# An even layer's pooling as products with band matrices, wider value chunks, work moved to ScalarE, parameters begun later

## The chip, the cores and the metric

The kernel runs on one core of a Trainium2 chip. Its time is the device time of one execution in microseconds (us), and the figure for a kernel is the median over runs. The core has a matrix engine (TensorE, PE in the rows; PEld is its loading of stationary matrices), VectorE (DVE), ScalarE (ACT), GpSimd (POOL) and SyncE (SP), which issues most transfers. Each engine works through its own list of instructions in order and waits on semaphores for the others. On-chip data lies in SBUF; matmuls write to PSUM.

## The reference, cut to what matters

The program is an even layer, an odd layer, a mixing layer (a Fourier part and a state space model, the ssm) and a mixture of experts. The change lies in the even layer, and in the preparation of the ssm's parameters, which runs in the background of the even layer.

```python
def even_layer(...):          # z = rmsnorm(h) @ ev_w_in, split in columns
    pooled = pool_mixer(za, ev_pool_w, scale)     # za: 768 columns
    ret = retention(rq, rk, rv)                   # 4 heads, keys of 128, values of 192
    mem = mem_attention(xq, mem_n, w_mem_kv)
    h + (concat(pooled, ret, mem) * silu(gate)) @ ev_w_out

def pool_mixer(u, w_grp, scale):                  # groups of 192 channels
    for gi, w in enumerate((2, 4, 8, 16)):        # mean over the last w tokens, minus the token
        lo = max(t + 1 - w, 0)
        outs.append((cs[:, 1:, sl] - cs[:, lo, sl]) / (t + 1 - lo) - uf[..., sl])
    y = einsum('bsgc,gcd->bsgd', stack(outs), w_grp) * scale

def retention(q, k, v):                           # q, k rotated by position
    att = (q @ k.T) * decay                       # causal, per head
    o = att @ v                                   # in the reference: in chunks with a carried state
    o = (o - mean(o)) * rsqrt(var(o) + EPS)       # over the 192 columns of a head
```

## The kernel before

The 512 tokens are four blocks of 128 (`NB`). Every fp32 operand is held as a pair, a rounded high part and the remainder: `split` (L300 and L301) takes the high part by a copy on ACT and the remainder by a subtraction on DVE, and `scaled_split` (L310 and L311) does so with a factor for each partition. A product of two pairs is three matmuls (`mm3`, L315 to L317). Weights stream in by `weight_piece`: SP fetches up to 1024 columns' worth (`wraw`), ACT makes the high part (L344), and DVE the low part (L346); while `share` is 2, in the retention, POOL makes the low part of every second piece.

`proj_t` makes 128 output channels for all 512 tokens (24 matmuls of 512 columns, stationary operand: weights). `proj_n` makes token-major results, block after block, each with one PSUM tile of the four named "mm"; two more are "acc" and two "tr".

The retention (`even_ret`) goes through four heads: rotary query, the products of the head before, rotary key, values, one step of an earlier output projection (`self.wait()`), scores. The values of a head are 192 columns, so `values(h)` runs four times. `products` collects two PSUM "acc" tiles, takes mean and variance on DVE, and normalises four parts from PSUM, each by L768 on DVE.

The pooling (`even_pool`) makes six tiles of 128 channels by `proj_t`, and for each one DVE adds shifted copies (L826: 2, 4, 8, 16 tokens), scales and subtracts (L831), mends the first 16 tokens (L834 and L835) and splits the result; then come gate tiles and the group products.

`ssm_params` is a generator. Each `tick()`, at the start of every projection, takes one of its steps: exponentials and angles on DVE (L1097 to L1142), and for eight groups of parameters products on POOL (L1292 to L1297) with DVE subtractions between them, right-hand sides `crhs` (L1281 to L1285 on POOL) and small matmuls (L1259). It is assigned to `self.bg` before the memory branch. What a step issues stands in each engine's list between the layer's own instructions: a scheduler places it by the order in which the program issues it and by the buffers that come free.

Of the kernel before, what the change touches and what calls it, by code (L numbers as in the profile page):

```python
# [12 lines left out]
ALU = mybir.AluOpType  # L13
# [11 lines left out]
GROUPS = 1 + BLOCKS // 2  # L25
SH_RET = 2
# [6 lines left out]
def chunk_list(spans, width=128):  # L33
# [10 lines left out]
    "za": chunk_list([(0, 768)]),  # L44
    "rq": chunk_list([(768, 1280)]),
    "rk": chunk_list([(1280, 1792)]),
    "rv": chunk_list([(1792, 2560)], 192),
# [60 lines left out]
POOL_WIN = (2, 4, 8, 16)  # L108
POOL_BLOCKS = []
# [15 lines left out]
def const_arrays():  # L125
# [13 lines left out]
    pc = np.zeros((P, 6, 16), np.float32)  # L139
    t = np.arange(16)  # L140
    for tl in range(6):
        for q in range(P):
            w = POOL_WIN[(tl * 128 + q) // 192]
            pc[q, tl] = np.float32(1.0) / np.minimum(t + 1, w).astype(np.float32)
    c["pcnt"] = pc
# [96 lines left out]
class K:  # L242
# [126 lines left out]
    def proj_n(self, w, name, i, u, evac, nblk=NB):  # L369
# [4 lines left out]
        for b in range(nblk):  # L374
            out = self.ps()
            s = slice(b * P, (b + 1) * P)
            for k in range(w.kt):
                self.mm3(out[:, :n], tuple(x[:, s] for x in u[k]), wt[k], k == 0, k == w.kt - 1)
            evac(b, out[:, :n], n)

# [271 lines left out]
    def even(self, before_end=None, aside=None):  # L652
# [53 lines left out]
    def even_ret(self, w, u, wo):  # L706
# [40 lines left out]
        def products(h):  # L747
# [32 lines left out]
        for h in range(4):  # L780
# [6 lines left out]
            values(h)  # L787
            self.wait()
            scores(h)
        self.wait(2)  # L790
# [4 lines left out]
    def even_pool(self, w, u):  # L795
        nc, a = self.nc, self.a
        v = nc.vector
        npb = len(POOL_BLOCKS)
        pw = []
        for b0 in range(0, npb, 4):  # L800
            n = min(4, npb - b0)
            hi, lo = self.split_new(self.load(a["ev_pw"][:, b0:b0 + n], [P, n, P]), [P, n, P])
            pw += [(hi[:, z], lo[:, z]) for z in range(n)]
        pcnt = self.load(a["pcnt"], [P, 6, 16])
        pooled, ys = {}, []
        done = 0

        def window(tl):
            o = self.proj_t(w, "za", tl, u)
            x = self.s([P, 16 + T])  # L810
            v.memset(x[:, :16], 0.0)
            v.tensor_tensor(x[:, 16:], o, self.rfull, ALU.mult)
            pend = []
            for q0 in (0, 64):
                win = POOL_WIN[(tl * 128 + q0) // 192]
                if pend and pend[0][2] == win:
                    pend[0] = (0, 128, win)
                else:
                    pend.append((q0, q0 + 64, win))
            res = self.s()  # L820
            cur, lvl, q0 = x, 1, 0
            maxw = max(p[2] for p in pend)
            while lvl < maxw:
                nxt = self.s([P, 16 + T])
                s0 = 2 * lvl - 1
                v.tensor_tensor(nxt[q0:, s0:], cur[q0:, s0:], cur[q0:, s0 - lvl:16 + T - lvl], ALU.add)  # L826
                lvl *= 2
                cur = nxt
                for (p0, p1, win) in list(pend):
                    if win == lvl:  # L830
# [1346 lines left out]
```

## Time and profile before

| | us |
|---|---|
| median of 3 runs | 2358.47 |
| lowest and highest | 2357.61, 2365.06 |
| profiled execution, its own time | 2362.91 |
| span of its trace | 2361.1 |
| PE busy in the span | 2131.4 |
| DVE, ACT, POOL busy | 1109.2, 661.2, 422.7 |

The span runs from the first to the last instruction. PE is busy for 90% of it. The even layer takes about the first 500 us; the rest is the other layers, which the change leaves as they are. The mean granted clock of PE in the profiled execution is 0.964 of full speed. The granted clock of a stretch (PEclk) is a mean of times at 1.2 and at 2.4 GHz; at the lower level a matmul takes about twice as long. A matmul's own duration overlaps with the next one's, so what a matmul costs in a stream is the distance from its start to the next one's start.

### The profile page before, as it was taken

How to read it: one execution, taken by the hardware profiler on the slowest of the kernel's cores; microseconds unless marked ns; L12 is line 12 of the kernel's file. 1: busy time of each engine (PE TensorE's matmuls, PEld its weight loads, DVE VectorE, ACT ScalarE, POOL GpSimd, SP SyncE). 2: the span in 40 equal slices, each digit the busy share in tenths (PEclk: the TensorE clock that was granted, in tenths of full speed). 3: DMA queues.
4: the chain of work that ended last, by engine and by line, in shares of the span. 5: the costliest groups of instructions: out<-in, count | busy, mean ns of one | idle time of the engine just before them, and what ended most of it. 6: DMA issues, size and time to landing. Idle time of an engine off the chain costs nothing. (4 is left out here: it accounts for less than half of the span.)

```text
span 2361.1 us, 30316 instructions
## 1 busy us (share of the span) xinstructions
PE 2131.4 (90%) x11350; PEld 1408.9 (60%) x11350; DVE 1109.2 (47%) x2229; ACT 661.2 (28%) x1289; POOL 422.7 (18%) x465
## 2 busy tenths in 40 slices
PE   7989998999999999999999988998787878887966
PEld 7878887787788888879777764433232323232311
DVE  7787869675446656666662634231111111111203
ACT  6623222344535645643224321000000000000001
POOL 1235755210014433421220210000000000000000
PEclk9989999899999999999999989999999999999988
DMA  5213334454232122114253489899999999999996
GB/s 183 94 59 108 116 100 138 141 167 152 72 102 64 38 73 72 43 59 137 90 163 108 152 333 381 339 392 426 427 427 426 427 426 427 427 427 427 427 426 252
DMA packets 110689, 545.85 MB, mean 231 GB/s; under 512 B 13664, under 2 KB 14605, under 8 KB 62410
## 3 DMA queue, kind: packets, MB, share of 16 engines
q1 hardware_dynamic: 105690, 529.14, 57.8%
q0 software_dynamic: 4528, 13.67, 1.7%
q8 instruction: 92, 1.51, 0.3%
q10 hardware_dynamic: 320, 1.05, 0.1%
q14 instruction: 59, 0.48, 0.1%
HBM read 530.70 MB, written 15.20 MB: 231 GB/s over the span
## 5 line engine op out<-in xcount | busy, mean ns | idle before, releaser
L2013 PE MATMUL mps<-ew,xt 128*32 128x512 f32 (+1 forms) x2048 | 383.4, 645 | 85.1 <-DMA ew<-in_w_up 47.9
L315 PE MATMUL ps<-uh,wh 128*128 128x512 f32 (+1 forms) x728 | 294.7, 405 | 7.8 <-ACT uh L310 7.0
L317 PE MATMUL ps<-uh,wl 128*128 128x512 f32 (+1 forms) x728 | 289.9, 398 | 5.1 <-DVE wl L346 5.1
L344 ACT ACTIVATE wh<-wraw 128x1024 fp32r<-128x1024 f32 (+5 forms) x187 | 186.8, 999 | 379.1 <-PE ps L316 267.5
L316 PE MATMUL ps<-ul,wh 128*128 128x512 f32 (+1 forms) x728 | 289.4, 398 | 0.5 <-DVE ul L311 0.5
L2013 PEld LDWEIGHTS mps<-ew,xt 128*32 128x32 f32 (+1 forms) x2048 | 86.5, 118 | 326.3 <-issue 170.7
L346 DVE TENSOR_TENSOR wl<-wraw,wh 128x1024 fp32r<-128x1024 f32 (+4 forms) x172 | 218.7, 1272 | 52.7 <-ACT wh L344 51.4
L2036 PE MATMUL mps<-ew,s 128*32 128x512 f32 (+1 forms) x960 | 173.9, 608 | 25.7 <-DMA ew<-in_w_down 13.9
L2099 POOL TENSOR_TENSOR ew<-x,ew 128x512 f32<-128x512 f32 x4 | 5.0, 1290 | 908.1 <-DMA ew<-in_w_down 908.1
L315 PEld LDWEIGHTS ps<-uh,wh 128*128 128x128 f32 (+1 forms) x728 | 137.2, 188 | 43.3 <-ACT uh L310 7.0
L317 PEld LDWEIGHTS ps<-uh,wl 128*128 128x128 f32 (+1 forms) x728 | 136.9, 188 | 40.0 <-DVE wl L346 6.0
L316 PEld LDWEIGHTS ps<-ul,wh 128*128 128x128 f32 (+1 forms) x728 | 137.2, 188 | 31.7 <-DVE ul L311 1.0
L1990 PE MATMUL mps<-s,hn 128*128 128x256 f32 (+1 forms) x576 | 135.0, 386 | 2.6 <-DVE s L1931 2.6
L1990 PEld LDWEIGHTS mps<-s,hn 128*128 128x128 f32 x576 | 104.4, 198 | 53.3 <-issue 33.5
L315 PE MATMUL ps<-yh,wh 128*128 128x512 f32 x320 | 130.8, 411 | 1.9 <-DVE s L311 1.9
L317 PE MATMUL ps<-yh,wl 128*128 128x512 f32 x320 | 128.4, 401 | 4.0 <-DVE wl L346 4.0
L2036 PEld LDWEIGHTS mps<-ew,s 128*32 128x32 f32 (+1 forms) x960 | 49.0, 113 | 137.6 <-issue 79.7
L2018 DVE SCALAR_TENSOR_TENSOR s<-mps,tab,s 128x512 f32<-128x512 f32 x17 | 12.8, 750 | 248.7 <-issue 153.3
L316 PE MATMUL ps<-yl,wh 128*128 128x512 f32 x320 | 129.0, 403 | 0.2
L1998 DVE TENSOR_SCALAR xt<-mps,gperm 128x256 f32<-128x256 f32 (+1 forms) x36 | 16.8, 468 | 237.2 <-PE mps L2013 198.3
L310 ACT ACTIVATE s<-mps,tab 128x512 fp32r<-128x512 f32 x34 | 23.4, 687 | 346.7 <-PE mps L2036 332.5
L311 DVE SCALAR_TENSOR_TENSOR s<-mps,tab,s 128x512 fp32r<-128x512 f32 x34 | 25.5, 751 | 188.4 <-ACT s L310 187.6
(517 smaller groups left out, 3962.7 us busy)
## 6 DMA issues: line engine op xcount, KB each, us to landing
ew<-in_w_gate SPq DMA_DIRECT2D x128, 1024.0 KB, 19.5
ew<-in_w_up SPq DMA_DIRECT2D x128, 1024.0 KB, 19.5
ew<-in_w_down SPq DMA_DIRECT2D x128, 1024.0 KB, 19.5
wraw<-in_od_w SPq DMA_DIRECT2D x44, 512.0 KB, 3.6
wraw<-in_ev_w SPq DMA_DIRECT2D x34, 512.0 KB, 3.5
wraw<-in_b_w SPq DMA_DIRECT2D x24, 512.0 KB, 3.5
b<-in_od_w SPq DMA_DIRECT2D x32, 256.0 KB, 4.3
wraw<-in_ev_wo SPq DMA_DIRECT2D x16, 384.0 KB, 3.3
```

The source lines that it names most:

```text
L310: self.nc.scalar.activation(hi, src, AF.Copy, scale=col)
L311: self.nc.vector.scalar_tensor_tensor(lo, src, col, hi, ALU.mult, ALU.subtract)
L315: mm(out, l[0], r[0], start=start, stop=False)
L316: mm(out, l[0], r[1], start=False, stop=False)
L317: mm(out, l[1], r[0], start=False, stop=stop)
L344: nc.scalar.activation(hi, raw, AF.Copy)
L346: (nc.gpsimd if on_pool else nc.vector).tensor_tensor(lo, raw, hi, ALU.subtract)
L1990: nc.tensor.matmul(tp[:, k * n:k * n + n], self.hn[:, b, k0 + k], one, start=i == 0, stop=i == len(sel) - 1)
L1998: nc.vector.tensor_scalar(t_[:, k], o, g, None, ALU.mult)
L2013: nc.tensor.matmul(o[rs], xt[k][:, c0 + z * m:c0 + z * m + m], self.expert_rhs(w[i][z], k, 512, 0, 512), start=k == 0, stop=k == KD - 1)
L2018: nc.vector.scalar_tensor_tensor(act, h[1], r, act, ALU.mult, ALU.mult)
L2036: self.nc.tensor.matmul(y[hf][rs], at[:, k, rs], self.expert_rhs(w[-1][r], k, D, hf * 512, 512), start=k == 0, stop=k == 3)
```

## The change

Values and pooling inputs come in chunks of 384 columns (two each, instead of four of 192 and six of 128). The new `proj_wide` keeps four PSUM tiles open, one for each token block, and takes each piece of weights through all of them; values are made at heads 0 and 2 alone, for two heads at a time. The pooling no longer adds shifted copies: a constant 128 by 144 matrix for each window holds the weights of the mean minus the token, and token-major inputs are multiplied by it (96 matmuls in all). The normalisation after the retention's products runs on ACT, as do the copies into `crhs` and the square in `sincos`. `ssm_params` is assigned to `self.bg` after the scores of head 0.

```diff
+BG_FROM = 0
...
-    "za": chunk_list([(0, 768)]),
+    "za": chunk_list([(0, 768)], 384),
     "rq": chunk_list([(768, 1280)]),
     "rk": chunk_list([(1280, 1792)]),
-    "rv": chunk_list([(1792, 2560)], 192),
+    "rv": chunk_list([(1792, 2560)], 384),
...
-    c["pcnt"] = pc
+    c["band"] = np.stack([np.stack([
+        np.where((j >= p) & (j < p + w), np.float32(1.0) / n.astype(np.float32), np.float32(0.0)) - (j == p)
+        for n in (np.full_like(j, w), np.minimum(j + 1, w))], 1) for w in POOL_WIN], 1).astype(np.float32)
...
+    def proj_wide(self, w, name, i, u, evac):
+
+        self.tick()
+        n = w.off[name, i][1]
+        step = 1024 // n
+        outs = [self.ps("acc"), self.ps("acc"), self.ps(), self.ps()]
+        for k0 in range(0, w.kt, step):
+            wt = self.weight_piece(w.src(name, i, k0, k0 + step)[0], step, n)
+            for k in range(k0, k0 + step):
+                for b in range(NB):
+                    self.mm3(outs[b][:, :n], tuple(x[:, b * P:b * P + P] for x in u[k]), wt[k - k0], k == 0,
+                             k == w.kt - 1)
+            self.tick()
+        for b in range(NB):
+            evac(b, outs[b][:, :n], n)
...
-        self.bg = aside and aside()
         self.fills.append(self.add_out(wo, 12, self.mem_branch(w, u, kv, 1, first)))
         self.share = SH_RET
-        self.even_ret(w, u, wo)
+        self.even_ret(w, u, wo, aside)
...
-            vp = [self.pair([P, 2, 192]) for _ in range(2)]
-            v[h] = [tuple(x[:, b % 2] for x in vp[b // 2]) for b in range(NB)]
+
+            vp = [self.pair([P, 2, 192]) for _ in range(NB)]
+            for j in range(2):
+                v[h + j] = [tuple(x[:, j] for x in vp[b]) for b in range(NB)]
 
             def evac(b, o, n):
-                self.scaled_split(*v[h][b], o, self.rcol[:, b:b + 1])
-            self.proj_n(w, "rv", h, u, evac)
+                self.scaled_split(*(x.rearrange("p j d -> p (j d)") for x in vp[b]), o, self.rcol[:, b:b + 1])
+            self.proj_wide(w, "rv", h // 2, u, evac)
...
             r = self.rsqrt(rr, [P, NB])
+            mr = self.small([P, NB], "ret_mr")
+            nc.vector.scalar_tensor_tensor(mr, mv[:, :, 0], -1.0, r, ALU.mult, ALU.mult)
             for b in range(NB):
-                nc.vector.tensor_scalar(rn[h // 2][b][:, h % 2 * 192:h % 2 * 192 + 192], outs[b], mv[:, b, 0:1],
-                                        r[:, b:b + 1], ALU.subtract, ALU.mult)
+                nc.scalar.activation(rn[h // 2][b][:, h % 2 * 192:h % 2 * 192 + 192], outs[b], AF.Identity,
+                                     bias=mr[:, b:b + 1], scale=r[:, b:b + 1])
...
                 gated(0)
-            values(h)
+            if h % 2 == 0:
+                values(h)
             self.wait()
             scores(h)
+            if h == BG_FROM:
+                self.bg = aside and aside()
         self.wait(2)
         products(3)
         self.wait(2)
...
-        pcnt = self.load(a["pcnt"], [P, 6, 16])
...
-        def window(tl):
-            o = self.proj_t(w, "za", tl, u)
-            x = self.s([P, 16 + T])
-            v.memset(x[:, :16], 0.0)
-            v.tensor_tensor(x[:, 16:], o, self.rfull, ALU.mult)
...
-            while lvl < maxw:
-                nxt = self.s([P, 16 + T])
-                s0 = 2 * lvl - 1
-                v.tensor_tensor(nxt[q0:, s0:], cur[q0:, s0:], cur[q0:, s0 - lvl:16 + T - lvl], ALU.add)
-                lvl *= 2
...
-                    if win == lvl:
-                        v.scalar_tensor_tensor(res[p0:p1], cur[p0:p1, 16:], 1.0 / win, x[p0:p1, 16:], ALU.mult,
-                                               ALU.subtract)
-                        hd = self.small([P, 16], "pool_h")
-                        v.tensor_tensor(hd[p0:p1], cur[p0:p1, 16:32], pcnt[p0:p1, tl], ALU.mult)
-                        v.tensor_tensor(res[p0:p1, :16], hd[p0:p1], x[p0:p1, 16:32], ALU.subtract)
...
-            pooled[tl] = self.split_new(res)
+        mm = nc.tensor.matmul
+        for c in range(2):
+            zp = [self.pair([P, 384]) for _ in range(NB)]
+
+            def evac(b, o, n):
+                self.scaled_split(*zp[b], o, self.rcol[:, b:b + 1])
+            self.proj_wide(w, "za", c, u, evac)
...
+            band = [self.split_new(self.load(a["band"][:, 2 * c + j], [P, 2, BAND]), [P, 2, BAND]) for j in range(2)]
             self.wait()
+            for t in range(3):
+                pooled.append(self.pair())
+                for q0, q1, j in ((0, P, t // 2),) if t != 1 else ((0, 64, 0), (64, P, 1)):
+                    o = self.ps()
+                    hi, lo = band[j]
+                    for b in range(NB):
+                        l, o_, n = tuple(x[:, t * P:t * P + P] for x in zp[b]), o[:, b * P:], min(BAND, T - b * P)
+                        if b == 0:
+                            self.mm3(o_[:, :n], l, (hi[:, 1], lo[:, 1]), True, False)
+                        else:
+                            mm(o_[:, 16:n], l[0], hi[:, 0, 16:n], start=False, stop=False)
+                            mm(o_[:, :16], l[0], hi[:, 0, :16], start=False, stop=False)
+                            mm(o_[:, :n], l[1], hi[:, 0, :n], start=False, stop=b == NB - 1)
+                    self.split(*(x[q0:q1] for x in pooled[t]), o[q0:q1])
+                self.tick()
+            for t in range(3 * c, 3 * c + 3):
+                g = self.gate_tile(w, t, u)
                 op = self.ps("acc")
...
+                need = [b for b in POOL_BLOCKS if b[1] == t]
+                for n, (i, _) in enumerate(need):
+                    self.mm3(op, pw[i, t], pooled[i - 3 * c], n == 0, n == len(need) - 1)
...
-        nc.vector.tensor_tensor(c, h, h, ALU.mult)
-        nc.vector.tensor_scalar(c, c, -2.0, 1.0, ALU.mult, ALU.add)
+        nc.scalar.activation(c, h, AF.Square)
+        nc.scalar.activation(c, c, AF.Copy, bias=1.0, scale=-2.0)
...
-                g_.tensor_copy(crhs[ds_, 0, :, d], cm[ds_, 0, gs])
-                g_.tensor_scalar(crhs[ds_, 1, :, d], cm[ds_, 1, gs], -1.0, None, ALU.mult)
+                nc.scalar.activation(crhs[ds_, 0, :, d], cm[ds_, 0, gs], AF.Copy)
+                nc.scalar.activation(crhs[ds_, 1, :, d], cm[ds_, 1, gs], AF.Copy, scale=-1.0)
```

The instruction lists move with it. In the first, on DVE, the stretch around the evacuation of the first values before (L311 with 128x192 out of PSUM; L1107, L1098, L1099, L1213, L1225 and L1142 belong to the parameters):

```order
L1141 TENSOR_TENSOR s_1333<-s_1332 128x256
L311 SCALAR_TENSOR_TENSOR s_1328<-ps_1352,rcol_338,s_1327 128x192
L1142 TENSOR_SCALAR s_1333<-s_1333 128x256
L1226 TENSOR_TENSOR pc_1077<-s_1333,s_1236 128x256
L311 SCALAR_TENSOR_TENSOR s_1328<-ps_1379,rcol_338,s_1327 128x192
L311 SCALAR_TENSOR_TENSOR s_1330<-ps_1406,rcol_338,s_1329 128x192
L1213 TENSOR_TENSOR s_1460<-x_702,idx_677 128x288
L1105 TENSOR_SCALAR s_1464<-s_1460 128x288
L1098 TENSOR_SCALAR s_1463<-s_1464 128x288
L1099 TENSOR_SCALAR s_1463<-s_1463 128x288
L1107 SCALAR_TENSOR_TENSOR s_1464<-s_1463,s_1464 128x288
```

and now (L310 is the same line of `scaled_split`, L528 the output projection's addition, L756 the scores' decay):

```order
L300 TENSOR_TENSOR s_1183<-s_1176,s_1182 128x512
L310 SCALAR_TENSOR_TENSOR s_1187<-ps_1194,rcol_338,s_1186 128x384
L310 SCALAR_TENSOR_TENSOR s_1189<-ps_1195,rcol_338,s_1188 128x384
L310 SCALAR_TENSOR_TENSOR s_1191<-ps_1196,rcol_338,s_1190 128x384
L345 TENSOR_TENSOR wl_1594<-wraw_1591,wh_1593 128x1024
L310 SCALAR_TENSOR_TENSOR s_1193<-ps_1197,rcol_338,s_1192 128x384
L528 TENSOR_TENSOR h_104<-ps_1332,h_104 128x512
L528 TENSOR_TENSOR h_106<-ps_1346,h_106 128x512
L756 TENSOR_TENSOR s_1366<-ps_1362,s_1360 128x512
L300 TENSOR_TENSOR s_1369<-s_1366,s_1368 128x512
L756 TENSOR_TENSOR s_1376<-ps_1372,s_1360 128x384
```

The parameters' instructions that stood between the evacuations are gone from this place; the four evacuations follow each other with one weight piece between them.

The second is POOL at one group of parameters, before (`crhs`, then the products; DMA rows are transfers that POOL issues):

```order
L1281 MEMSET crhs_2950 128x256
L1284 COPY crhs_2950<-bc_1854 64x4x16
L1285 TENSOR_SCALAR crhs_2950<-bc_1854 64x4x16
L1284 COPY crhs_2950<-bc_1854 64x4x16
L1285 TENSOR_SCALAR crhs_2950<-bc_1854 64x4x16
L1292 TENSOR_TENSOR mat_2956<-pc_1077,bb_934 128x8x4x16
L1295 TENSOR_TENSOR mat_2957<-ps_1078,bb_934 128x8x4x16
L1274 DMA ssm_win_665<-s_2865 128x512
L1274 DMA ssm_win_665<-s_2873 128x512
L346 TENSOR_TENSOR wl_3113<-wraw_3110,wh_3112 128x768
L1293 TENSOR_TENSOR s_2958<-ps_1078,bb_934 128x8x4x16
```

and now (line numbers are one lower):

```order
L1280 MEMSET crhs_3293 128x256
L1280 MEMSET crhs_3459 128x256
L1291 TENSOR_TENSOR mat_3465<-pc_1887,bb_1727 128x8x4x16
L1294 TENSOR_TENSOR mat_3466<-ps_1888,bb_1727 128x8x4x16
L1292 TENSOR_TENSOR s_3301<-ps_1888,bb_1727 128x8x4x16
L1295 TENSOR_TENSOR s_3302<-pc_1887,bb_1727 128x8x4x16
L1296 TENSOR_TENSOR mat_3300<-mat_3300,s_3302 128x512
L1291 TENSOR_TENSOR s_3354<-pc_1887,bc_2248 128x8x4x16
L1292 TENSOR_TENSOR s_3356<-ps_1888,bc_2248 128x8x4x16
L1294 TENSOR_TENSOR s_3355<-ps_1888,bc_2248 128x8x4x16
L1295 TENSOR_TENSOR s_3357<-pc_1887,bc_2248 128x8x4x16
```

The four copies into `crhs` and the transfers and the weight piece that stood between the products are not there; nine products of two groups follow each other.

## Rows read from the trace of the kernel before

**Rows 1.** Page, busy time of the engines, share of the span, instructions.

```profile
PE 2131.4 (90%) x11350; PEld 1408.9 (60%) x11350; DVE 1109.2 (47%) x2229; ACT 661.2 (28%) x1289; POOL 422.7 (18%) x465
```

**Rows 2.** Windows; from:to, length, busy us of each engine, PEclk, DMA.

```profile
110.00:160.00 50.00, 42.96 (x235) 36.63 (x234) 41.60 (x91) 12.35 (x21) 10.59 (x7) 0.90 0.24 75
160.00:210.00 50.00, 48.16 (x274) 42.15 (x273) 43.70 (x82) 12.85 (x21) 20.42 (x16) 0.97 0.24 75
260.00:310.00 50.00, 45.76 (x264) 39.36 (x263) 35.80 (x69) 14.05 (x23) 37.16 (x38) 0.90 0.35 116
340.00:380.00 40.00, 33.03 (x161) 26.57 (x160) 38.91 (x42) 8.71 (x13) 25.66 (x30) 0.96 0.32 106
420.00:460.00 40.00, 40.00 (x184) 32.86 (x183) 25.05 (x45) 11.77 (x18) 17.62 (x29) 0.87 0.57 154
```

**Rows 3.** Timeline of PE; start, us, instruction, [idle before it, releaser].

```profile
43.09 0.35 PE L315 MATMUL ps<-wh,s 128*128 128x256 f32 x1 [2.17 <-DVE th L1132]
...
141.63 0.69 PE L315 MATMUL ps<-s,s 128*128 128x384 f32 x1 [4.12 <-DVE s L311]
...
294.77 3.62 PE L1259 MATMUL ps<-crhs,mat 128*128 128x32 f32 x16 [4.02 <-DVE s L768]
...
374.77 0.50 PE L317 MATMUL ps<-yh,wl 128*128 128x512 f32 x1 [4.02 <-DVE wl L346]
...
416.52 1.58 PE L875 MATMUL ps<-s,rel 33*12 33x512 f32 x2 [2.26 <-issue]
```

**Rows 4.** Timeline of DVE around the first values' evacuation.

```profile
134.82 2.54 DVE L1107 SCALAR_TENSOR_TENSOR s<-s,s 128x288 f32<-128x288 f32 x1
...
138.33 2.92 DVE L1113 SCALAR_TENSOR_TENSOR s<-s,s 128x288 f32<-128x288 f32 x6
141.17 0.41 DVE L311 SCALAR_TENSOR_TENSOR s<-ps,rcol,s 128x192 fp32r<-128x192 f32 x1
```

**Rows 5.** Timeline of DVE and of POOL, 341 and 366 us.

```profile
341.23 7.95 DVE L831 SCALAR_TENSOR_TENSOR s<-s,s 128x512 f32<-128x512 f32 x1
...
366.38 8.34 DVE L346 TENSOR_TENSOR wl<-wraw,wh 128x768 fp32r<-128x768 f32 x1
...
366.51 1.07 POOL L1293 TENSOR_TENSOR s<-ps,bb 128x512 f32<-128x512 f32 x1
...
372.85 1.05 POOL L1296 TENSOR_TENSOR s<-pc,bc 128x512 f32<-128x512 f32 x1
```

**Rows 6.** Timeline of PE, matmuls following each other.

```profile
115.85 0.25 PE L315 MATMUL ps<-wh,uh 128*128 128x192 f32 x1
...
123.75 0.27 PE L317 MATMUL ps<-wh,ul 128*128 128x192 f32 x1
...
145.24 0.63 PE L316 MATMUL ps<-ul,wh 128*128 128x512 f32 x1
145.67 0.63 PE L317 MATMUL ps<-uh,wl 128*128 128x512 f32 x1
...
149.40 0.40 PE L315 MATMUL ps<-uh,wh 128*128 128x512 f32 x1
149.63 0.39 PE L316 MATMUL ps<-ul,wh 128*128 128x512 f32 x1
...
324.16 1.87 PE L1259 MATMUL ps<-crhs,mat 128*128 128x32 f32 x16
...
718.32 0.34 PE L315 MATMUL ps<-s,b 128*128 128x384 f32 x1
...
719.73 0.34 PE L317 MATMUL ps<-b,s 128*128 128x384 f32 x1
```

**Rows 7.** Source groups; ns min/median/max, first and last start us, forms.

```profile
L768 DVE TENSOR_SCALAR s<-ps,ret_mv,rs_y x16: 466/469/480, 159.8 to 295.0; 128x192 f32<-128x192 f32 x16
L1284 POOL COPY crhs<-bc x16: 229/268/737, 96.1 to 384.3; 64x64 f32<-64x64 f32 x16
L1285 POOL TENSOR_SCALAR crhs<-bc x16: 367/374/912, 96.8 to 384.9; 64x64 f32<-64x64 f32 x16
```

More of the change, by code (lines that the diff above doesn't have):

```diff
@@ L108 @@
 POOL_WIN = (2, 4, 8, 16)
+BAND = P + 16
 POOL_BLOCKS = []
@@ L138, in const_arrays @@
     c["decay"] = dec.astype(np.float32)
[L139 to L144, printed above, removed]
-    c["pcnt"] = pc
+    p, j = np.arange(P)[:, None], np.arange(BAND)[None, :]
+    c["band"] = np.stack([np.stack([
+        np.where((j >= p) & (j < p + w), np.float32(1.0) / n.astype(np.float32), np.float32(0.0)) - (j == p)
+        for n in (np.full_like(j, w), np.minimum(j + 1, w))], 1) for w in POOL_WIN], 1).astype(np.float32)
     fr = np.arange(128)[:, None] < 64
@@ L704, in even, with even_ret @@
             pass
-    def even_ret(self, w, u, wo):
+    def even_ret(self, w, u, wo, aside):
         nc, a = self.nc, self.a
@@ L796, in even_pool @@
         nc, a = self.nc, self.a
[L797 to L803, printed above, removed]
-        pcnt = self.load(a["pcnt"], [P, 6, 16])
-        pooled, ys = {}, []
-        done = 0
-        def window(tl):
-            o = self.proj_t(w, "za", tl, u)
-            x = self.s([P, 16 + T])
-            v.memset(x[:, :16], 0.0)
-            v.tensor_tensor(x[:, 16:], o, self.rfull, ALU.mult)
[L813 to L822, printed above, removed]
-            while lvl < maxw:
-                nxt = self.s([P, 16 + T])
-                s0 = 2 * lvl - 1
-                v.tensor_tensor(nxt[q0:, s0:], cur[q0:, s0:], cur[q0:, s0 - lvl:16 + T - lvl], ALU.add)
-                lvl *= 2
-                cur = nxt
-                for (p0, p1, win) in list(pend):
-                    if win == lvl:
-                        v.scalar_tensor_tensor(res[p0:p1], cur[p0:p1, 16:], 1.0 / win, x[p0:p1, 16:], ALU.mult,
-                                               ALU.subtract)
-                        hd = self.small([P, 16], "pool_h")
-                        v.tensor_tensor(hd[p0:p1], cur[p0:p1, 16:32], pcnt[p0:p1, tl], ALU.mult)
-                        v.tensor_tensor(res[p0:p1, :16], hd[p0:p1], x[p0:p1, 16:32], ALU.subtract)
-                        pend.remove((p0, p1, win))
-                        if pend:
-                            q0 = pend[0][0]
-            pooled[tl] = self.split_new(res)
-            self.wait()
@@ L842, in even_pool @@
-        window(0)
-        for tl in range(6):
-            if tl < 5:
-                window(tl + 1)
-            while done < 6:
-                need = [b for b in POOL_BLOCKS if b[1] == done]
-                if max(i for i, _ in need) > tl:
-                    break
-                g = self.gate_tile(w, done, u)
+        mm = nc.tensor.matmul
[4 more added lines that the diff above has]
+            self.proj_wide(w, "za", c, u, evac)
+            nums = [n for n, (_, o) in enumerate(POOL_BLOCKS) if o // 3 == c]
+            pw, pooled, ys = {}, [], []
+            for b0 in range(nums[0], nums[-1] + 1, 4):
+                n = min(4, nums[-1] + 1 - b0)
+                hi, lo = self.split_new(self.load(a["ev_pw"][:, b0:b0 + n], [P, n, P]), [P, n, P])
+                for z in range(n):
+                    pw[POOL_BLOCKS[b0 + z]] = hi[:, z], lo[:, z]
+            band = [self.split_new(self.load(a["band"][:, 2 * c + j], [P, 2, BAND]), [P, 2, BAND]) for j in range(2)]
+            self.wait()
+            for t in range(3):
[15 more added lines that the diff above has]
+                g = self.gate_tile(w, t, u)
@@ L851, in even_pool @@
                 op = self.ps("acc")
-                for n, (i, oo) in enumerate(need):
-                    self.mm3(op, pw[POOL_BLOCKS.index((i, oo))], pooled[i], n == 0, n == len(need) - 1)
-                ys.append(self.put_y(op, g, self.gcols[:, 24 + done:25 + done]))
+                need = [b for b in POOL_BLOCKS if b[1] == t]
+                for n, (i, _) in enumerate(need):
+                    self.mm3(op, pw[i, t], pooled[i - 3 * c], n == 0, n == len(need) - 1)
+                ys.append(self.put_y(op, g, self.gcols[:, 24 + t:25 + t]))
@@ L855, in even_pool @@
                 self.wait()
-                done += 1
-                if done % 3 == 0:
-                    yield ys
-                    ys = []
+            yield ys
     def odd_setup(self):
```

## The prediction

> **What bounds the kernel now.** I read the page's busy times first: PE is busy for 2131.4 of 2361.1 us and no other engine for more than half [rows 1], so outside waits on PE the time is the length of PE's own stream. The change ends with the even layer, so I then cut its 500 us into windows and looked where PE is not busy or its clock is low [rows 2]. Two things are read from such a row. Idle time is the window less PE's busy time: 50 − 42.96 = 7.04 us at 110 to 160 us. And a mean granted clock of 0.90 means that a fifth of the 50 us ran at the lower level (1.2 of 2.4 GHz), of which half would have been spared: 0.10 × 50 = 5.0 us. In that way the windows hold, as idle and as clock loss:
>
> 110 to 160 (first values): 7.04 + 5.0 = 12.0 us. 160 to 210 (products): 1.84 + 1.5 = 3.3. 260 to 310 (last products): 4.24 + 5.0 = 9.2. 340 to 380 (pooling): 6.97 + 1.6 = 8.6. 420 to 460: 0 + 5.2 = 5.2.
>
> Then the timeline of PE, for what ended each wait [rows 3]. At 141.63 it had waited 4.12 us for DVE's L311, the evacuation of the values. DVE was busy for 41.60 of those 50 us, and just before it ran the parameters' exponentials, L1107 for 2.54 and six L1113 for 2.92 us, so that the evacuation started at 141.17 [rows 4]: queued, not slow (0.41 us). At 294.77 the parameters' matmuls waited 4.02 us for a PSUM "acc" tile which L768, the normalisation, held. At 374.77 PE waited 4.02 us for L346, the low part of a weight piece. That one L346 took 8.34 us while POOL ran seven products from 366.51 to 373.90, and at 341.23 one L831 of the pooling took 7.95 us in the same way [rows 5]. So both operations were held until POOL's run ended, and that is not the work that they do.
>
> **The change, part by part.**
>
> *PE's stream.* What a matmul costs is the pitch in a full stream [rows 6]. 512 columns at the upper clock: 149.63 − 149.40 = 0.23 us; at the lower: 145.67 − 145.24 = 0.43. 192 columns: (123.75 − 115.85)/71 = 0.111. 384 columns: (719.73 − 718.32)/8 = 0.176. Values: 384 matmuls of 192 columns (4 heads × 4 blocks × 8 × 3) were 42.6 us; now 192 of 384 columns, 33.8: −8.8. Pooling inputs: 144 of 512 columns were 33.1; now 192 of 384, 33.8: +0.7. Bands: 96 new matmuls of 144 columns or fewer. None like them is in the trace; 32 columns cost 1.87/16 = 0.117 and 192 cost 0.111, so narrow matmuls cost about the same whatever their width. I take 0.111: +10.7 (bounds: by columns alone 144/512 of 0.23 is 0.065, 6.2 in all; as 512 columns, 22). Together +2.6.
>
> On the bands a rule speaks for less. The Trainium skill, "TensorE: Matmul & The Clock Gate", section "Back-to-back issue gap", gives about 81 ns for a matmul of 128 columns with its weight load in a stream; an estimate by it is 96 × 0.081 = 7.8 us. The rows at 0.111 and 0.117 disagree with it here, and the sum goes by the rows.
>
> *Values without the parameters between.* ssm_params is begun after head 0's scores, so no exponential stands between the evacuations (the first excerpt of DVE's list), and two of four values stages vanish. Of the 12.0 us at 110 to 160 I take 10; the other 2 stay for PSUM tiles that all four evacuations hold at once. The wait at 43.09 (2.17 us, L1132 belongs to the parameters) goes too, with a little clock behind it: 2.5.
>
> *Products.* The four L768 of a head (16 × 0.469 = 7.5 us of DVE in all [rows 7]) go to ACT, which is busy for 14.05 of the 50 us around the last ones [rows 2]. Of 9.2 us at 260 to 310 I take 3.5, nearly the wait of 4.02: ACT's four now hold the same "acc" tiles, after the same statistics, and the slow stretch that follows is one of narrow matmuls. At 160 to 210 I take 1 of 3.3, because a new wait comes in: with no values stage at heads 1 and 3, only the 24 matmuls of one output-projection step (24 × 0.23 = 5.5 us) lie between rotary key and scores, while behind a key stand four rotary operations and a split on DVE and ACT; at 0.41 us for 192 columns [rows 4], and up to 1.1 for 512, I estimate 3 to 6 us for them.
>
> *Pooling.* DVE loses its shifted additions, L831 and the small mends; it was busy for 38.91 of 40 us there [rows 2], and one of the two operations that were held leaves with them. Of 8.6 I take 5. In their place stand two stages (one per chunk) in which PE waits for the first pooled input: four evacuations, then the bands, whose splits queue on DVE behind the pool weights' and the parameters' work, while some 10 us of PE work are ready as cover. The nearest rows bound each at 0 and at 4.02 + 1.6 = 5.6 us (a held DVE operation and the clock lost in its window). I take 1.5 each, nearer the covered end: +3.
>
> *At no cost.* The `crhs` copies (16 × (0.27 + 0.37) us on POOL [rows 7]), the squares and the normalisations add to ACT, which is busy for a third of any window here [rows 2]; its other duty, the weights' high parts, runs pieces ahead. Without that cover each piece would be late by some 0.5 us. The parameters end no later against the even layer's end, since they still have the whole retention from head 1 and the pooling. At 420 to 460 the loss stays: the clock falls after the gap before L875 at 416.52, which waits for nothing that the change touches.
>
> *Sum.* PE +2.6; waits and clock −10 −2.5 −3.5 −1 −5 = −22; new waits +3: −16.4 us. From the profiled 2362.91 that is 2346.5. That execution is 4.44 above the median of 2358.47, which gives **2342** us.
>
> **The rivals.**
>
> *A. All of it goes.* If nothing takes the place of what held PE, the four windows and the wait at 43.09 are recovered whole: 12.0 + 3.3 + 9.2 + 8.6 + 2.5 = 35.6. Then 2.6 − 35.6 = −33.0, or 2325.5. For it: every one of these waits names DVE, and DVE loses work in each. Against it: the parameters' work is moved, not removed, and POOL's runs get longer. The Trainium skill, "SBUF — State Buffer", section "SBUF: two separate sides", says that VectorE and GpSimd share a port pair that one instruction locks while the other engine waits; by it a held operation would be late by one POOL product. The trace has 8.34 us for one held operation against 1.07 for one product [rows 5], so here the hold went through the whole run, which speaks against this rival. 0.17.
>
> *B. The waits move.* The parameters' DVE work goes from the first values into heads 1 to 3 and the pooling. Only the first stage's 12.5 are gained, and one more wait like that at 374.77 comes in (5.6): 2.6 − 12.5 + 3 + 5.6 = −1.3, or 2357. For it: of DVE's 1109 us only the pooling's and the normalisation's operations leave, and what PE waited for was always queued behind DVE's other work. 0.16.
>
> *C. Denser POOL runs, slower.* Without the copies into `crhs`, and with transfers moved, POOL's products of two groups follow each other (the second excerpt: nine in a row, where before four copies, two transfers and a weight piece broke them). Each run holds whatever DVE operation meets it, and now splits for bands and weights meet it, with PE right behind. The place is the second half of the retention and the pooling; a hold costs 5.6 us as at 374.77. On the base of B without its one hold (−6.9) the kernel is slower by more than 0.3% from the third hold on; with four it is −6.9 + 22.4 = +15.5, or 2374. For it: seven groups come with such a run. Against it: in the trace of before most holds fell on operations which PE did not need at once. 0.12.
>
> **How the numbers follow.** The forecast has 0.55, A 0.17, B 0.16, C 0.12. A measurement of this kernel can tell about 0.3% (7 us, its three runs lie 7.5 apart) from no change. The forecast, with half to all of its 22 us and up to twice 5.6 for the new waits, spans 2334 to 2352; A lies below, B within 0.3%, C above. So faster has 0.55 + 0.17 = 0.72, but some of the forecast's upper end is within 0.3%: 0.71; same 0.17; slower 0.12. The range goes from a little under A to just over B, 2323 to 2360, and leaves out most of C and a tail of A.
>
> **What would show it.** In the profile after: PE's idle time between rotary key 0 and scores 0 falls to about 2 us, and the clock there stays near 1; 384-column matmuls of the values at 0.176 pitch; band matmuls at about 0.11; no PE wait of 4 us on the normalisation; PE busy time about 2 us higher at an equal clock. Step by step wrong: a PE wait over 3 us ahead of the first band or pooled product, of scores 1 or 3, or on a weight's L346 next to a POOL run (C); DVE operations of 5 us and more from 200 us on that PE waits for; any PE wait released by ACT's normalisation. The prediction is wrong as a whole if the even layer's last matmul comes less than 8 us earlier, or if the odd layer's stream, which has the same instructions, changes its length.

## The result: slower by 1.4%

The changed kernel takes 2393.93 us (2391.18 to 2395.76) against 2358.04 for the kernel before in the same runs: a ratio of 1.0142, interval 1.012 to 1.0164, or 33 us where 16 less were forecast. The page and a few landmarks say where. First, the page of the kernel after, to hold against [rows 1]:

```profile
PE 2148.2 (90%) x11302; PEld 1433.9 (60%) x11302; DVE 1078.6 (45%) x2159; ACT 687.2 (29%) x1358; POOL 408.1 (17%) x433
```

The normalisation of the last products (L768 [rows 7], L786 after) is the end of the retention, the last addition of the output projection (L513, L528 after) is that of the even layer, and a line at the end of the odd layer (L1340, L1339 after) marks what follows. Timeline of ACT and DVE and source group, after:

```profile
286.57 1.72 ACT L786 ACTIVATE s<-ps,ret_mr,rs_y 128x192 f32<-128x192 f32 x4 [9.67 <-DVE ret_mr L784]
...
522.46 0.68 DVE L528 TENSOR_TENSOR h<-ps,h 128x512 f32<-128x512 f32 x1
...
L1339 DVE SCALAR_TENSOR_TENSOR s<-s,gf,s x7: 739/743/1786, 1078.9 to 1096.8; 128x512 f32<-128x512 f32 x7
```

and before:

```profile
293.85 1.25 DVE L768 TENSOR_SCALAR s<-ps,ret_mv,rs_y 128x192 f32<-128x192 f32 x3
...
489.82 0.68 DVE L513 TENSOR_TENSOR h<-ps,h 128x512 f32<-128x512 f32 x1
...
L1340 DVE SCALAR_TENSOR_TENSOR s<-s,gf,s x7: 737/746/1779, 1047.6 to 1065.5; 128x512 f32<-128x512 f32 x7
```

The last four normalisations begin at 286.57 instead of 293.85, so the retention ends 7.3 us earlier; the even layer ends 32.6 us later, the prediction's sign of being wrong as a whole, while the odd layer keeps its length (556.4 us, before 557.8) and the span is 32.2 longer. So by the time stamps all of the loss lies between the first two, in the pooling and what runs beside it. The whole even layer, after and then before (columns as in [rows 2]):

```profile
0.00:522.50 522.50, 471.18 (x2462) 408.13 (x2463) 353.29 (x641) 216.35 (x386) 195.21 (x193) 0.92 0.35 110
...
0.00:489.80 489.80, 454.14 (x2503) 384.58 (x2504) 382.59 (x709) 189.71 (x315) 209.69 (x224) 0.96 0.36 117
```

Of the 32.7 us, 15.7 are idle time of PE (51.32 against 35.66) and 17.0 are its busy time. The mean granted clock falls from 0.96 to 0.92; read as the prediction reads its windows, that is some 42 us of clock loss against 20. The two overlap, since part of the idle time is at the lower level, but the slower matmuls cost about as much as the waits. The windows, after:

```profile
110.00:160.00 50.00, 50.00 (x262) 44.30 (x261) 36.05 (x67) 17.82 (x28) 10.02 (x5) 1.00 0.31 98
160.00:210.00 50.00, 47.17 (x237) 40.65 (x236) 37.09 (x82) 18.67 (x36) 12.81 (x10) 0.97 0.27 79
210.00:260.00 50.00, 38.25 (x176) 32.58 (x174) 42.54 (x82) 13.40 (x24) 24.45 (x19) 0.90 0.25 77
260.00:310.00 50.00, 43.72 (x214) 36.94 (x215) 35.36 (x59) 15.83 (x29) 33.12 (x30) 0.86 0.32 103
310.00:360.00 50.00, 43.75 (x285) 40.28 (x283) 32.90 (x42) 18.60 (x39) 28.50 (x32) 0.90 0.38 123
...
410.00:460.00 50.00, 37.83 (x228) 34.34 (x226) 26.64 (x38) 15.06 (x28) 19.02 (x24) 0.75 0.37 116
```

The first values' 12 us are gone, as forecast: PE busy for all of 110 to 160 at the full clock. They are back at 210 to 260, head 2's values: 11.75 us idle and 5.0 of clock, where before had this:

```profile
210.00:260.00 50.00, 48.81 (x345) 44.32 (x343) 39.58 (x69) 16.37 (x26) 37.94 (x35) 1.00 0.35 111
```

Over 110 to 260, idle time and clock loss are 21 us, where they were 16.5. And at 410 to 460 DVE is busy for only 26.64 us, yet PE is idle for 12.17 and loses 12.5 to the clock. Timeline of PE, the waits after (the first is the one of [rows 3] at 43.09 again):

```profile
43.66 0.36 PE L314 MATMUL ps<-wh,s 128*128 128x256 f32 x1 [2.18 <-DVE th L1131]
...
219.24 0.69 PE L315 MATMUL ps<-wl,uh 128*128 128x384 f32 x1 [6.74 <-DVE wl L345]
...
287.54 0.85 PE L1258 MATMUL ps<-crhs,mat 128*128 128x32 f32 x3 [5.38 <-ACT s L786]
...
341.36 1.97 PE L1258 MATMUL ps<-crhs,mat 128*128 128x32 f32 x16 [2.52 <-DVE s L310]
...
354.08 0.70 PE L314 MATMUL ps<-s,s 128*128 128x144 f32 x2 [3.34 <-ACT s L299]
...
364.80 0.45 PE L847 MATMUL ps<-s,s 128*128 128x128 f32 x1
...
429.74 3.62 PE L1258 MATMUL ps<-crhs,mat 128*128 128x32 f32 x16 [4.44 <-DVE s L310]
...
454.65 0.70 PE L314 MATMUL ps<-s,s 128*128 128x144 f32 x2 [7.21 <-ACT s L299]
```

Three different queues stand behind the longest of these. At 219 it is DVE's: the parameters' exponentials stand ahead of a piece of the values' weights. At 430 a DVE operation of the parameters is held through POOL products, as in [rows 5], their sine on ACT waits for it, and the evacuation stands behind the sine. At 455 it is SP's: the band load stands behind a weight piece that waits for DVE's L345. Timeline of DVE, POOL, ACT and SP, after:

```profile
214.34 2.44 DVE L1113 TENSOR_SCALAR s<-s 128x288 f32<-128x288 f32 x1
...
217.88 0.44 DVE L1112 SCALAR_TENSOR_TENSOR s<-s,s 128x288 f32<-128x288 f32 x1
218.25 0.94 DVE L345 TENSOR_TENSOR wl<-wraw,wh 128x768 fp32r<-128x768 f32 x1
...
419.14 6.12 DVE L1131 SCALAR_TENSOR_TENSOR s<-s,s 128x512 f32<-128x512 f32 x1
...
419.57 1.08 POOL L1295 TENSOR_TENSOR s<-pc,bb 128x512 f32<-128x512 f32 x1
...
424.79 1.60 POOL L1296 TENSOR_TENSOR s<-s,s 128x512 f32<-128x512 f32 x1
...
426.75 0.63 ACT L1138 ACTIVATE s<-s 128x512 f32<-128x512 f32 x1 [4.95 <-DVE s L1132]
...
428.47 0.56 ACT L309 ACTIVATE s<-ps,rcol 128x384 fp32r<-128x384 f32 x1
...
447.81 1.21 DVE L345 TENSOR_TENSOR wl<-wraw,wh 128x1024 fp32r<-128x1024 f32 x1
...
449.04 0.33 SPq L338 DMA_DIRECT2D wraw<-in_ev_w  x1
449.55 1.19 SPq L320 DMA_DIRECT2D s<-in_band  x2
...
454.15 0.44 ACT L299 ACTIVATE s<-s 128x288 fp32r<-128x288 f32 x1 [7.72 <-DMA ssm_k<-kx]
454.98 0.44 ACT L299 ACTIVATE s<-s 128x288 fp32r<-128x288 f32 x1 [0.38 <-DMA s<-in_band]
```

L345 ends at 449.02, the piece is issued at 449.04, the band load at 449.55, and ACT splits the band at 454.15 (the row names another transfer as the last; the next row names the band's).

### The profile page after: what moved, and what is told of

Same layout as the page of the kernel before. It is cut to its first block, busy times and chain, and to the rows that moved or that the text cites. A ratio compares the mean times of both kernels' runs of the same rounds, so it can differ in the third digit from the quotient of the medians.

```text
span 2393.3 us, 30186 instructions
## 1 busy us (share of the span) xinstructions
PE 2148.2 (90%) x11302; PEld 1433.9 (60%) x11302; DVE 1078.6 (45%) x2159; ACT 687.2 (29%) x1358; POOL 408.1 (17%) x433
## 5 line engine op out<-in xcount | busy, mean ns | idle before, releaser
L343 ACT ACTIVATE wh<-wraw 128x1024 fp32r<-128x1024 f32 (+2 forms) x189 | 187.4, 992 | 380.6 <-PE ps L315 287.6
L314 PE MATMUL ps<-uh,wh 128*128 128x512 f32 x680 | 277.3, 408 | 11.4 <-ACT uh L309 7.5
L315 PE MATMUL ps<-ul,wh 128*128 128x512 f32 x680 | 273.0, 402 | 0.5 <-DVE ul L310 0.5
L316 PE MATMUL ps<-uh,wl 128*128 128x512 f32 x680 | 273.4, 402 | 0.0
L345 DVE TENSOR_TENSOR wl<-wraw,wh 128x1024 fp32r<-128x1024 f32 (+2 forms) x174 | 212.3, 1221 | 49.7 <-ACT wh L343 48.1
L314 PEld LDWEIGHTS ps<-uh,wh 128*128 128x128 f32 x680 | 130.0, 191 | 45.6 <-ACT uh L309 7.5
L316 PEld LDWEIGHTS ps<-uh,wl 128*128 128x128 f32 x680 | 129.5, 191 | 32.5 <-issue 1.0
L315 PEld LDWEIGHTS ps<-ul,wh 128*128 128x128 f32 x680 | 129.7, 191 | 30.1 <-DVE ul L310 1.0
L1997 DVE TENSOR_SCALAR xt<-mps,gperm 128x256 f32<-128x256 f32 (+1 forms) x36 | 16.8, 468 | 239.9 <-PE mps L2012 200.8
L2017 DVE SCALAR_TENSOR_TENSOR s<-mps,tab,s 128x512 f32<-128x512 f32 x17 | 12.8, 750 | 248.2 <-issue 155.1
L309 ACT ACTIVATE s<-mps,tab 128x512 fp32r<-128x512 f32 x34 | 23.4, 687 | 346.4 <-PE mps L2035 332.0
L1007 POOL TENSOR_SCALAR s<-s,n_sm 128x128 f32<-128x128 f32 (+3 forms) x96 | 110.8, 1173 | 7.2 <-DVE n_sm L998 3.9
```

Of the source, the lines that this page charges most:

```text
L309: self.nc.scalar.activation(hi, src, AF.Copy, scale=col)
L314: mm(out, l[0], r[0], start=start, stop=False)
L315: mm(out, l[0], r[1], start=False, stop=False)
L316: mm(out, l[1], r[0], start=False, stop=stop)
L343: nc.scalar.activation(hi, raw, AF.Copy)
L345: (nc.gpsimd if on_pool else nc.vector).tensor_tensor(lo, raw, hi, ALU.subtract)
```

## The experiments

Ratios are to the kernel before in the same runs; 0.001 is 2.4 us. "Step" means one step of the parameters' generator, taken by a `tick()`.

**The parts alone.** Kernel before with one part of the change each: `only_band` (za chunks and `even_pool`), `only_bg` (begin moved), `only_wide` (rv chunks, `values` and `proj_wide`), `only_act` (normalisation, squares, `crhs`); the edits are those parts of the diff.

> The kernel before with the pooling alone changed (wide za chunks and band matrices). Theory Q (bands late): the band matrices' loads stand on SP behind a weight piece that waits for its buffer, PE waits ahead of the bands (3.3 and 7.2 us in the changed kernel), and the narrow matmuls after it run at the low clock: 20 to 35 us slower than before, 2378 to 2393, with two PE waits released by ACT's L299 on the bands. Rival P (parameters begun later are what hurts the pooling): about 5 to 12 us slower, the bands' own matmuls at 0.11 us, since here the parameters are begun early. Rival W (the wide projections' hold on the PSUM acc tiles): waits on L310 ahead of the parameters' small matmuls, some 10 us.

1.0159 (1.014 to 1.0177), 2394.47 us. The waits of 3.35 and 6.59 us ahead of the bands are there with early parameters too, so the late start doesn't make them. The loss, 37 us, is over Q's 35, and rival W's wait is there as well (5.45 us on L310 ahead of the parameters' small matmuls).

> The kernel before with the parameters begun after head 0's scores and nothing else. Theory Q: the waits at the first values go and some come back later, between 8 us faster and 3 us slower. Rival P: 15 us slower or more, with held DVE operations in the pooling that PE waits for.

1.0071 (1.0053 to 1.0089): slower, P's sign and size. (The trace of this run is of its fastest execution, 2365.79 us, 8 under its median; that of `late_act` below is 5.5 under.)

> The kernel before with the values in chunks of 384 through the wide projection and nothing else. The retention of the changed kernel ended 7.2 us earlier than before; PE's stream loses 8.8 us by pitch. Theory Q: 5 to 10 us faster. Rival W (the wide projection's open PSUM tiles and fewer stages to cover scores): no gain or slower, with waits of 3 us and more ahead of scores 1 and 3 and on the second chunk's weights.

1.0133 (1.0113 to 1.0154): no gain at all, as rival W says. Timeline of DVE and PE at the first scores of `only_wide` (L1134 and L1137 are the parameters' exponentials, L531 the output projection's addition, which frees the PSUM tile that scores want):

```profile
142.53 2.85 DVE L1134 SCALAR_TENSOR_TENSOR s<-s,s 128x288 f32<-128x288 f32 x1
145.30 1.36 DVE L1137 TENSOR_SCALAR s<-s 128x288 int32<-128x288 int32 x1
146.58 2.01 DVE L1134 SCALAR_TENSOR_TENSOR s<-s,s 128x288 f32<-128x288 f32 x2
...
150.01 0.68 DVE L531 TENSOR_TENSOR h<-ps,h 128x512 f32<-128x512 f32 x1
...
150.84 0.77 PE L317 MATMUL ps<-s,s 128*128 128x512 f32 x1 [12.05 <-DVE h L531]
```

> The kernel before with the normalisation, the squares and the crhs copies on ACT and nothing else. Theory Q: within 4 us of before. Rival C of the prediction (denser runs on POOL hold DVE): 8 us slower or more, with more DVE operations of 5 us and above than before.

0.9973 (0.9959 to 0.9987), 2349.84 us: faster than both kernels. But the trace does not show the gain where the change works. PE's wait ahead of the parameters' matmuls at the last products is 3.98 us instead of 4.02, now released by ACT. The largest thing that is gone is the gap ahead of L875 ([rows 3], 2.26 us) and the lower clock behind it ([rows 2], 0.87 at 420 to 460). Window of `only_act`:

```profile
420.00:460.00 40.00, 40.00 (x179) 32.53 (x178) 25.71 (x43) 12.74 (x18) 16.24 (x27) 1.00 0.62 173
```

That is worth 2.26 + 5.2 = 7.5 of the 12.8 us between the two traces, and the execution traced before lay 4.4 us above its median. Why the gap closes, and whether it is there in every execution of the kernel before, is not shown. The parts sum to +0.0336, the whole is 0.0142, so they are no independent terms.

**Mending the pooling.** Bands and pool weights ahead of the projection (the diffs of this part are shortened):

```diff
+            nums, pw, band = ...        # the same lines, moved up
             self.proj_wide(w, "za", c, u, evac)
-            nums, pw, band = ...
```

> The changed kernel with the band matrices and the pool weights loaded and split ahead of the wide projection instead of behind it. Theory Q (late bands): the waits of 3.3 and 7.2 us ahead of the bands go, the bands run at 0.11 instead of 0.21 us each (9 us less for 96) and the matmuls behind them keep the upper clock: 18 to 24 us less than the changed kernel, 2370 to 2376. Rival N (narrow matmuls lower the clock by themselves): only the waits go, 8 to 11 us, 2383 to 2386, and the bands stay at 0.2 us.

1.0136 (1.0116 to 1.0156), no clear gain. The first wait on the bands is gone, but not the slow bands: behind a wait of 1.36 us and 32 narrow matmuls of the parameters from 341.27 on, the first 48 took (354.80 − 344.91)/47 = 0.210 us each. Window of these bands:

```profile
344.91:354.80 9.89, 9.89 (x49) 9.89 (x47) 4.94 (x7) 3.45 (x8) 9.81 (x10) 0.50 0.36 132
```

And at 437.69 PE waits 9.96 us for the evacuation L309, again behind a held DVE operation (L1098, 5.67 us) and the sine. Then, with PSUM:

```diff
-        outs = [self.ps("acc"), self.ps("acc"), self.ps(), self.ps()]
+        outs = [self.ps() for _ in range(NB)]          # for za alone
```

> As band_early, and the wide projection of the pooling inputs takes four of the PSUM tiles named mm and none of acc, so that the parameters' small matmuls need not wait for its evacuation. Theory W (the open acc tiles): the waits of 2.5 and 4.4 us ahead of L1258 go with the slow matmuls behind them, 7 to 12 us less than band_early. Rival: the four mm tiles make other projections wait instead, no gain.

1.0088 (1.0071 to 1.0105), 13 us under the changed kernel. The wait ahead of the parameters' small matmuls is gone in the first stage and is 8.43 us at 434.56 in the second, so theory W's waits are only half of the account. Here the bands run after a full stream. Timeline of PE, first and last of 48:

```profile
347.67 0.23 PE L314 MATMUL ps<-s,s 128*128 128x144 f32 x1
...
352.83 0.31 PE L847 MATMUL ps<-s,s 128*128 128x128 f32 x1
```

(352.83 − 347.67)/47 = 0.110 us each, against (364.80 − 354.08)/47 = 0.228 in the changed kernel behind its wait. Windows of these two stretches, `band_early_mm` and the changed kernel:

```profile
347.67:352.83 5.16, 5.16 (x48) 5.16 (x47) 2.90 (x4) 2.02 (x6) 5.16 (x6) 1.00 0.21 83
...
354.08:364.80 10.72, 10.32 (x48) 10.12 (x48) 9.92 (x10) 2.06 (x4) 10.30 (x10) 0.50 0.08 31
```

Interleaved, on acc and on mm tiles:

```diff
+            for t in range(3):
+                gs.append(self.gate_tile(w, 3 * c + t, u))      # ahead of the bands of t
```

> As band_early, with the gate projection of each pooling tile placed ahead of its bands instead of behind all of them, so that 24 wide matmuls stand between the groups of narrow ones. Rival N: the clock stays up and the bands go to about 0.11 us each, 6 to 12 us less than band_early. Theory Q: within 3 us of band_early, since once the bands are there nothing waits.

1.0091 (1.0074 to 1.0107): 11 us less than `band_early`, as rival N says; the first tiles' groups of bands run at 0.104 to 0.108 us each.

> The changed kernel with all three mendings of the pooling: bands loaded early, the pooling inputs' PSUM tiles all mm, the gate projections between the groups of bands. Bands early on mm tiles ran at 0.109 us each and gave 16 us, the interleaving on acc tiles 15 us. Theory K (what the bands lose is the lower clock after a wait, and both mendings spare the same waits): 2374 to 2379, about the same. Rival (they add): 2366 to 2372.

1.0065 (1.0048 to 1.0082): 18 us gained by all three, more than K, less than the sum. And the same mended pooling on `only_act`, parameters early:

> The three mendings of the pooling with the values of before and the parameters begun early: work on ACT and bands alone. From work on ACT alone (2350): the bands' own matmuls add 11 us of PE time, and the shifted additions leave DVE. Theory K: 2350 to 2362. Rival P (the late start was the larger part of what the mended kernel still loses): 2345 to 2352. If the bands lose by something else than the waits: over 2370.

1.0053 (1.0036 to 1.0069), 19 us over `only_act`: even mended, the new pooling loses to the shifted additions. Whether by its bands or by the five steps in each of its wide projections no run separates. At 434.82 PE waits 8.02 us for an evacuation behind ACT's L299, which waits for a band load (3.61 us): loads placed early in the program still queue on SP.

**Without the bands.** Pooling of before in the changed kernel:

> The changed kernel with the pooling of before (shifted additions on DVE, six tiles of 128). If the pooling holds all of the loss, as the time stamps say (retention ends 7.2 us earlier than before, the even layer 31 us later), this is 0 to 8 us faster than before, 2349 to 2357. Rival P (late parameters hurt any pooling, as the run with the later start alone was 17 us slower): 5 to 15 us slower than before.

1.0044 (1.0028 to 1.0061): the new pooling (bands, wide projection and its steps) is 0.0098, 23 us, of the loss; 10 us are in the rest. The time stamps alone had misled: the retention's gain comes back in any pooling.

**Steps and start.** One step for each wide projection, on early parameters and in the changed kernel:

```diff
                              k == w.kt - 1)
-            self.tick()
         for b in range(NB):
```

> The kernel before with the work on ACT and the wide values, parameters begun early, and one background step per chunk of values (none between its weight pieces). The wide values alone, with five steps per chunk, were 31 us slower; the work on ACT alone 6.4 faster. Theory T (the five steps put the parameters' DVE work between the values' weight pieces and ahead of the additions that scores wait for): the loss goes, 2340 to 2350. Rival V (the open PSUM tiles and the missing stage between rotary key and scores): still 15 us slower or more, 2370 to 2385.

1.0007 (0.9993 to 1.0021). `only_wide` was 1.0133, and the work on ACT gives 0.0027, so the steps cost about 0.010, 23 us, if these two parts add; the wide values with one step are still 8 us slower than `only_act`.

> The changed kernel with one background step for each wide projection instead of five. Theory T (the steps between the weight pieces put the parameters' DVE work ahead of the pieces and evacuations that PE needs: 6.7 us at 219, the held evacuation at 430): 12 to 22 us less than the changed kernel, 2372 to 2382. Rival E (the parameters then end too late and the even layer waits for them): no gain or slower, 2390 to 2400, with small matmuls of the parameters after 460 us.

1.0061 (1.0038 to 1.0085): 19 us of the changed kernel's loss go with that one line. The waits at 219, 341 and 430 are gone, and the second one on the bands is 1.80 us instead of 7.21. Windows of `after_1tick`:

```profile
210.00:260.00 50.00, 41.63 (x193) 34.48 (x193) 37.75 (x84) 15.52 (x27) 17.74 (x13) 0.90 0.28 86
...
410.00:460.00 50.00, 48.20 (x260) 42.21 (x259) 32.24 (x42) 18.55 (x36) 36.24 (x38) 0.86 0.33 109
```

Most of the gain lies in the pooling: idle time and clock loss at 410 to 460 fall from 24.7 to 8.8 us, those at head 2 only from 16.8 to 13.4, where smaller waits took the place of the one at 219.

> The changed kernel with the crhs copies back on POOL. Rival C of the prediction (without the copies POOL's products run in one piece and hold DVE longer): 8 us less or more, under 2386, and no DVE operation of over 5 us next to the evacuation at 430. Theory T: within 4 us of the changed kernel, 2390 to 2398, since on the kernel before the copies' place made no difference.

1.015 (1.0127 to 1.0174), no change, and the wait at 430 is there (4.45 us): the copies' place is not the cause. On the kernel before (`act_no_crhs`) neither:

> The kernel before with the normalisation and the squares on ACT, the crhs copies left on POOL. Work on ACT with the copies was 6.4 us faster. If rival C of the prediction holds (POOL's denser runs cost), this is faster still, 2340 to 2347. If the copies' place doesn't matter: 2348 to 2352. If it is POOL's relief that gains: 2353 to 2358.

0.9971 (0.9957 to 0.9985).

> The kernel before with the work on ACT and the parameters begun after head 0's scores; values and pooling as before. Early, this was 6.4 us faster than before. Theory P (the late start is what costs the changed kernel its 10 us without bands): 2362 to 2372. Rival: late start and wide values cost only together, 2348 to 2356.

1.0049 (1.0032 to 1.0067), 18 us over `only_act` for moving one line. Timeline of DVE and PE of `late_act`; this is [rows 4] and the second of [rows 3] again, 75 us later, at head 2's values:

```profile
212.89 2.92 DVE L1134 SCALAR_TENSOR_TENSOR s<-s,s 128x288 f32<-128x288 f32 x6
215.73 0.41 DVE L313 SCALAR_TENSOR_TENSOR s<-ps,rcol,s 128x192 fp32r<-128x192 f32 x1
...
216.19 0.80 PE L317 MATMUL ps<-yh,wh 128*128 128x512 f32 x1 [5.29 <-DVE s L313]
```

Its parameters' last small matmuls come at 462.7 us, against 416.5 in `only_act`. An earlier and a half-late start (three `tick()` after the begin; the begin ahead of the retention):

> The kernel before with the work on ACT and the parameters begun three steps earlier instead of later, so that their exponentials come in the memory branch and not between the first values. If what the late start was to gain is the 12 us at the first values, this gains up to that without squeezing the rest: 2338 to 2346. Rival: the exponentials stall the memory branch instead, 2350 to 2360.

0.9997 (0.9985 to 1.001): the rival, 5.46 us of wait at 314 and 3.77 at 130 in place of the first values'.

> The kernel before with the work on ACT and the parameters begun ahead of the retention, one stage later than before and one head earlier than in the change. Theory P (whatever values stage the exponentials fall into waits behind them, and a later start squeezes the end): they now fall into head 1's, so nothing is gained at the first and the end is a little later: 2350 to 2360. Rival (a short delay is free): 2340 to 2347.

1.008 (1.0062 to 1.0098): worse than either expectation, 25 us over `only_act` for a begin that lies one stage later.

> The changed kernel with the three mendings of the pooling (bands early, mm tiles, gate projections between) and one background step for each wide projection. One step alone gave 22 us, the mendings alone 20. Still there with one step: waits of 3.3 and 1.8 us ahead of the bands, bands at 0.22 us (10 us over their price at the upper clock). Theory T with late bands: about 10 us less than after_1tick, 2358 to 2364. If both spare the same waits: 2368 to 2373. If they add: 2350 to 2355.

1.0125 (1.0106 to 1.0145): neither; the mendings cost 15 us here. Source group and window of `fix_1tick`:

```profile
L1259 PE MATMUL ps<-crhs,mat x128: 191/276/401, 304.5 to 481.9; 128*128 128x32 f32 x128
...
510.00:560.00 50.00, 42.37 (x233) 36.22 (x232) 23.70 (x50) 15.15 (x20) 1.17 (x1) 0.90 0.60 198
```

The parameters end at 482 us (469.2 in `after_1tick`, 446.6 in the changed kernel, 424.7 before), and PE is idle for 7.6 us where the odd layer begins. Whether the later end is what costs the 15 us is not shown.

## Why the prediction was wrong

The step that failed is the gain of 10 at the first values, with the move that was to bring it put under "At no cost". The 12 us at 110 to 160 did go, but the parameters' work did not leave PE's path: the same exponentials now stand ahead of head 2's weights (6.74 us at 219) or, in `late_act`, of its evacuation (5.29 us), and 110 to 260 together hold 4.5 us more than before. On `only_act` the move alone costs 18 us, on the kernel before 17. The reason that was given, that "the parameters end no later against the even layer's end", held in the changed kernel: their small matmuls end at 446.6 of 522.5 us, before at 424.7 of 489.8. The end was the wrong thing to look at; what counted here is the stages into which the work falls. Nor did the prediction count the five steps of `proj_wide`, which issue DVE, ACT and POOL work between the pieces of weights: one step instead of five gives 19 us back.

The 2.5 for the wait at 43.09 came to nothing: PE waits 2.18 us at the same place. The scheduler puts the parameters' first operations (128 by 32) there in both kernels, although `self.bg` is assigned only after head 0's scores; the move delays the later steps alone.

The second step that failed is "+3" for new waits in the two stages of the pooled input, with "some 10 us of PE work" as cover. They were 2.52 + 3.34 and 4.44 + 7.21, 17.5 in all, 7.0 of them ahead of the parameters' small matmuls and 10.6 ahead of the bands; the second stage alone is twice the bound of 5.6. The cover was weighed for the splits on DVE, and not for SP and ACT: a load behind a weight piece, an evacuation behind a sine that itself waits for a held DVE operation.

PE's stream was right by its price (0.110 against 0.111) and wrong by its clock: at the lower level the bands ran at 0.228, so the 48 of the first stage alone took 10.7 us, what the sum gave to all 96. The prediction kept that as its upper bound, 22.

The products' 3.5 did not come either: the wait for the normalisation is 5.38 us, released by ACT, instead of 4.02, and 3.98 with the work on ACT alone. In that part's trace the largest gain is the closed gap ahead of L875, where the prediction said that the loss stays. The pooling's −5 did not come: DVE got free and PE waited for others.

Rival B had the mechanism (the waits move with the parameters) and priced it at one wait of 5.6. Rival C had the sign; a hold of its kind is at 419.14, but the copies that it rests on do nothing (`after_crhs`). Rival A fell. What the prediction read in [rows 5], that a hold lasts through many POOL products, came again: L1131 took 6.12 us while five products of 1.06 to 1.08 followed each other, and ended 0.5 us after the sixth instruction of that run began, at 424.79.

Open stays why the parts don't add (`fix_1tick`, `act_mid`): each moves the parameters against the stages, and no run held that alignment fixed while changing one part. One stage's shift alone was worth 25 us (`act_mid`), so the prices of 18 to 23 us hold for the kernel on which each was measured. The late start is the clearest case: on narrow values it costs 18 us, but wide values are at 1.0133 with early parameters and at 1.0044 with late ones and the work on ACT (`all_but_band`). The changed kernel with an early start was not run, so what the late start costs in it is not known. A kernel with all bands resident on chip from the start was not tried.

## What to carry to other kernels

Background work that a loop releases step by step is part of every stage that releases it: count the steps that an edit adds or drops, and ask which queue each of their instructions stands in, and ahead of what. A wait ahead of a stage of narrow matmuls was paid twice here, once idle and once at the lower clock. And an in-order queue that feeds a new stage (a load behind a weight piece, an evacuation behind a sine) mattered more here than the engine that was relieved.

The best version found is the change's smallest part, the work on ACT alone: 2349.84 us, 0.9973 of before and 0.983 of the changed kernel (`act_no_crhs`, without the copies, is its equal). Its gain is measured, and its cause is open.

## What the runs showed that was not expected

Matmuls of 16 to 144 columns took 0.110 us each in a stretch whose granted clock was 1.00, and 0.228 in one at 0.50 behind a wait of 3.34 us. PE was busy for 10.32 of that stretch's 10.72 us, and the clock stayed at the lower level (1.2 GHz) through all 48; the wide matmuls behind them started at it.
